# Layer 0's feed-forward in two-block form: nine of 22 up pairs as seven products, down sums carried over four parts

## The chip, the core and the metric

The kernel runs on one core of one Trainium2 chip. The metric is the device time of one execution in microseconds. A core has five engines that this text names as the profile does: PE is TensorE (matmuls; PEld is its weight load, which overlaps them), DVE is VectorE, ACT is ScalarE, POOL is GpSimd, and SP is SyncE, which issues nearly all DMAs here. Every engine works through its own instructions in a fixed order and waits on semaphores of the others.

## What is computed

Two model blocks in a row, on 256 tokens of width 1024. The change is in the second block's first layer, in its feed-forward, which runs over 512 tokens: 256 latent ones (tiles 0 and 1 of 128) and 256 of the context (tiles 2 and 3). Cut to that:

```python
def ada_norm(x, g, shift, scale):
    return rms_norm_2(x, g) * (1.0 + scale) + shift

def swiglu_ffn(h, w_in, w_out):
    a, g = jnp.split(h @ w_in, 2, axis=-1)
    return (jax.nn.silu(a) * g) @ w_out
...
    for i in range(DEPTH_2):
        mod_l = (silu_c @ ada_w[i] + ada_b[i])[:, None, :]
        mod_c = (silu_cc @ ada_w[i] + ada_b[i])[None, None, :]
        sh1_l, sc1_l, g1_l, sh2_l, sc2_l, g2_l = jnp.split(mod_l, N_MOD, axis=-1)
        ...
        h = h + g2_l * swiglu_ffn(ada_norm(h, norm_ffn[i], sh2_l, sc2_l), ffn_w_in[i], ffn_w_out[i])
        if ctx_out:
            hc = hc + g2_c * swiglu_ffn(ada_norm(hc, norm_ffn[i], sh2_c, sc2_c), ffn_w_in[i], ffn_w_out[i])
```

`w_in` is 1024 x 5632 and `w_out` is 2816 x 1024, so there are 22 pairs of up tiles (128 columns of `a` and the same 128 of `g`). The context's second half of a layer is needed in layer 0 alone.

## The kernel before, in words

**Numbers.** A product of float32 values is made from three matmuls of float32r values (`mm3`, lines 192 to 195): each operand is split into a rounded high part and the rest, and high x high, low x high and high x low are summed in PSUM. Weights come from DRAM in units of 128 x 1024 (512 KB) in one list, `UNITS`, in the order of their use. `w_load` (line 147) sends a unit into one of 5 `raw` buffers, `w_split` (line 161) makes `wh` on ScalarE (line 178) and `wl` on VectorE (line 179) in two of 12 `w` tiles, and `wnext` (line 181) hands the next unit out and keeps up to `cap` units split ahead.

**Layer 0's feed-forward.** It goes in two parts of 11 pairs. For each pair `ffn_up` (line 1122) runs 2 x 8 x 3 matmuls with a weight tile as the stationary operand and 512 tokens as the moving one, into two PSUM banks, and `ffn_act` (line 1109) makes silu(a) * g and splits it. The first two pairs (`ffn_up_first`, line 1132) do the context's half first, while the latent tokens are still being normed. `ffn_down0` (line 1149) then multiplies the part's 11 tiles by `w_out`, per output half and token tile, in a PSUM bank each, and `gated` (lines 1078 to 1081) multiplies a bank by the gate and adds it to the residual on VectorE. In part 0 all four token tiles go through one pass over the weights; in part 1 tiles 2 and 3 go first and tiles 0 and 1 in a second pass, so that the context's norm (`normed`, line 216, `to_T`, line 222) and layer 1's keys and values can begin early.

**The conditioning.** `ada_jobs` (line 293) computes the rows `silu(c) @ ada_w`, one vector of 1024 after the other, in 8 steps per vector: a DMA of 512 KB into one of two `a` buffers (line 304), and one pass of VectorE over it for each condition (line 324; for both c and c_ctx in layer 0 and for layer 1's first two, for c alone after). A vector's end adds the bias on GpSimd (line 339); the gate vectors (numbers 2 and 5) are also transposed on TensorE (line 348), sent to DRAM and read back as rows. The steps are strewn through the program by `ada_run`. The generator `adaC` holds the vectors (0,5), (1,0), (1,1) for both conditions and (1,3), (1,4), (1,2), (1,5) for one: 24 steps and 32.

**What sets the order.** In this stage the tile scheduler of the framework orders the instructions of every engine when the program is built. On the chip each engine then keeps to that order: an instruction that waits holds up all that stand behind it on its engine.

Of the kernel before, what the change touches and what calls it, by code (L numbers as in the profile page):

```python
# [14 lines left out]
ALU = mybir.AluOpType  # L15
# [12 lines left out]
NFT = FH // P  # L28
HALF = NFT // 2

# [6 lines left out]
def _units():  # L37

    u = [("f", "w_in", P * f) for f in range(8)]
    u += [("r", "w_in", k, 1024) for k in range(KD)]
    u += [("h", "w_in", 2 * k, 2048 + 512 * h) for h in range(2) for k in range(4)]
    u += [("r", "w_out", k, 0) for k in range(KD)]
    u += [("h", "ff1", 2 * k, 0) for k in range(4)] + [("f", "ff1", P * 4)]
    for f in range(NF):  # L50
        if 5 <= f + 2 < NF:
            u.append(("f", "ff1", P * (f + 2)))
        u.append(("r", "ff2", f, 0))
    v0 = [("h", "na_qkv", 2 * k, 2048) for k in range(4)]
# [6 lines left out]
    for part in range(2):  # L61
        for f in range(part * HALF, (part + 1) * HALF):
            u += [("f", "ffn_in0", P * f), ("f", "ffn_in0", FH + P * f)]
        dn = [("h", "ffn_out0", part * HALF + f, 512 * h) for h in range(2) for f in range(0, HALF, 2)]
        u += dn if part == 0 else dn + dn
# [18 lines left out]
def net(ctx, tc, x, xt, small, gk_up, gk_b, g_onorm, wst, final_norm, ctx_in, ctx_t, ada, ada_b, cvec,  # L84
# [76 lines left out]
    def w_split(upto):  # L161
        while wpos[1] < min(upto, len(UNITS)):
            i = wpos[1]
            raw = raws.pop(i)
            n = 512 if UNITS[i][0] == "h" and UNITS[i][1] == "ffn_out0" and (UNITS[i][2] % HALF) == HALF - 1 else 1024
            h = sb.tile([P, 1024], F32R, tag="w", bufs=NW, name=nm("wh"))
# [10 lines left out]
            else:  # L177
                A.copy(out=h[:, :n], in_=raw[:, :n])  # L178
                V.tensor_tensor(out=l[:, :n], in0=raw[:, :n], in1=h[:, :n], op=ALU.subtract)  # L179

    def wnext(kind):
        i = wpos[2]
# [9 lines left out]
    def mm3(o, lh, ll, rh, rl, first, last):  # L192
        T.matmul(o, lhsT=lh, rhs=rh, start=first, stop=False)  # L193
        T.matmul(o, lhsT=ll, rhs=rh, start=False, stop=False)  # L194
        T.matmul(o, lhsT=lh, rhs=rl, start=False, stop=last)  # L195

# [28 lines left out]

    def to_T_steps(xns, dst, t0, scale=None, bias=None):

        n = P * len(xns)
        for k in range(KD):
# [12 lines left out]
            else:  # L242
                r = t2([n])
                if k % 2:
# [31 lines left out]

    def mm_h(o, u, j, xp, t, first, last):
        h, l = u
        c = slice(j * 512, (j + 1) * 512)
        mm3(o, xp[0][:, t * P:(t + 1) * P], xp[1][:, t * P:(t + 1) * P], h[:, c], l[:, c], first, last)  # L280

# [818 lines left out]

    fT = new_T2()
    o_half(1, 2, hc, 1)
    xn = [normed(t) for t in hc]
    o_half(0, 0, lat, 0)
    o_half(1, 0, lat, 0, lambda: to_T(xn, fT, S, mod(0, 1, 4), mod(0, 1, 3)))
    xn = [normed(t) for t in lat]
# [14 lines left out]

    def ffn_up(L, src, n):
        ps_ = []
        for _ in range(2):
            u = wnext(("f", f"ffn_in{L}"))
            o = bank()
            for k in range(KD):
                mm_f(o[:, :n], u, src, k, 0, n, k == 0, k == KD - 1)
            ps_.append(o)
        return ffn_act(*ps_, n)  # L1130

    def ffn_up_first(src):

        us, os_ = [], []
        for _ in range(4):
            us.append(wnext(("f", "ffn_in0")))
            os_.append(bank())
            for k in range(KD):
                mm_f(os_[-1][:, S:N2], us[-1], src, k, S, S, k == 0, k == KD - 1)
        to_T(xn, src, 0, mod(0, 0, 4), mod(0, 0, 3))  # L1140
        z = []
        for n in range(4):
            for k in range(KD):
                mm_f(os_[n][:, 0:S], us[n], src, k, 0, S, k == 0, k == KD - 1)
            if n % 2:
                z.append(ffn_act(*os_[n - 1:n + 1], N2))
        return z

    def ffn_down0(hf, uu, tiles, between=None):
        ac = {t: bank() for t in tiles}  # L1150
        for f2 in range(0, HALF, 2):
            u = wnext(("h", "ffn_out0"))
            for j in range(min(2, HALF - f2)):
                f = f2 + j
                for t in tiles:
                    mm_h(ac[t], u, j, uu[f], t, f == 0, f == HALF - 1)
            ada_run(adaC)
            if f2 == 4 and between is not None:
                between()
        for t in tiles:  # L1160
            gated((lat + hc)[t], ac[t], 0, t // 2, 5, hf)

# [17 lines left out]

    for part in range(2):
        uu = []
        for f in range(HALF):
            if part == 0 and f < 2:
                uu += ffn_up_first(fT) if f == 0 else []
            else:
                uu.append(ffn_up(0, fT, N2))
            ada_run(adaC, 2)
        if part == 0:
            load_gates(0, 5)  # L1190
            for hf in range(2):
                ffn_down0(hf, uu, (2, 3, 0, 1))
        else:
            for hf in range(2):
                ffn_down0(hf, uu, (2, 3))
# [315 lines left out]

    load_gates(1, 5)
    nfb = [t2([512]) for _ in range(2)]
# [120 lines left out]
def _stream(w):  # L1634

    a = np.zeros((len(SLOT), P, 1024), np.float32)
    for s, i in SLOT.items():
# [9 lines left out]
        else:  # L1647
            k, c = s[2], s[3]
            n = 1 if s[1] == "ffn_out0" and k % HALF == HALF - 1 else 2
            a[i].reshape(P, 2, 512)[:, :n] = m[k * P:(k + n) * P, c:c + 512].reshape(n, P, 512).transpose(1, 0, 2)  # L1650
    return a
# [47 lines left out]
```

## Time and profile before

| | before |
|---|---|
| median of 3 runs | 1257.45 us (1257.27 to 1258.41) |
| the profiled execution | 1256.72 us |
| its span, first to last instruction | 1254.9 us |
| mean granted TensorE clock | 0.999 |
| layer 0's feed-forward, from its first matmul to layer 1's first | 557.8 to about 933.3 us of the span |

Times within a profile count from the span's start. In groups of instructions, what stands before the bar is what the instruction writes and reads, with its shape and count; behind it are the busy time in us, the mean of one in ns, the idle time of the engine just before, and what ended that. In a timeline a row starts with its start and its length in us. A matmul's printed length contains its way through the array, so that following ones overlap; the distance of their starts is what one takes.

### The profile page before, as it was taken

What the parts mean: (1) busy time and instruction counts of PE and PEld (TensorE: products, weight loads), DVE (VectorE), ACT (ScalarE), POOL (GpSimd) and SP (SyncE); (2) the same over time, 40 slices, a digit from 0 to 9 for tenths busy, and PEclk for the clock granted to TensorE, in tenths of its full rate; (3) what the DMA queues carried; (4) which work ended last, traced back from release to release, by engine and by line L of the source; (5) the groups of instructions that cost most, each with busy time, mean ns of one, the idle gap of its engine ahead of it and who ended that gap; (6) DMA issues with size and microseconds to landing.
All of it is one profiled execution on the core that took longest, in us unless ns stands there. A gap on an engine that the chain in (4) does not pass through costs nothing.

```text
span 1254.9 us, 18667 instructions
## 1 busy us (share of the span) xinstructions
PE 1244.0 (99%) x6872; PEld 1043.2 (83%) x6872; DVE 919.9 (73%) x1638; ACT 688.2 (55%) x1344; POOL 78.7 (6%) x137
## 2 busy tenths in 40 slices
PE   9999999999999999999999999999999999999997
PEld 8888889898888777789888888887888777999997
DVE  6959888697989887777877767633667988655555
ACT  8575655666549888655232222323456897544443
POOL 1010000030100000001000000000003220000000
PEclk9999999999999999999999999999999999999999
DMA  8647687787673333463656877633662324656650
GB/s 304 189 151 237 192 289 268 271 277 246 198 249 111 105 110 118 160 197 118 213 177 206 259 266 249 205 100 102 197 204 76 113 84 131 219 187 185 186 185 34
DMA packets 68507, 231.22 MB, mean 184 GB/s; under 512 B 8048, under 2 KB 8736, under 8 KB 68416
## 3 DMA queue, kind: packets, MB, share of 16 engines
q1 hardware_dynamic: 68128, 229.68, 57.0%
q8 instruction: 54, 0.88, 0.3%
q10 hardware_dynamic: 288, 0.35, 0.1%
q14 instruction: 37, 0.30, 0.1%
HBM read 228.93 MB, written 1.07 MB: 183 GB/s over the span
## 4 chain that ended last, share of the span: by engine, by line
PE 95%; ACT 2%; DVE 1%; issue 1%; DMA 0%; POOL 0%; SPq 0%; POOLq 0%; ACTq 0%
PE b L193 28%; PE b L194 28%; PE b L195 28%; PE b L1000 2%; PE b L1469 1%; PE b L981 1%; PE b L232 1%; PE b L1455 1%; PE b L562 1%; PE b L962 1%; PE b L963 1%; PE b L951 1%; PE b L1436 1%; DVE wl L179 0%; DMA t<-in_xt_dram 0%
## 5 line engine op out<-in xcount | busy, mean ns | idle before, releaser
L178 ACT CAST wh<-raw 128x1024 fp32r<-128x1024 f32 (+1 forms) x308 | 320.7, 1045 | 392.8 <-PE b L194 292.4
L179 DVE TENSOR_TENSOR wl<-raw,wh 128x1024 fp32r<-128x1024 f32 (+1 forms) x308 | 372.5, 1216 | 154.9 <-ACT wh L178 151.9
L193 PE MATMUL b<-t,wh 128*128 128x256 f32 (+1 forms) x1120 | 365.7, 327 | 0.0
L194 PE MATMUL b<-t,wl 128*128 128x256 f32 (+1 forms) x1120 | 365.6, 327 | 0.0
L195 PE MATMUL b<-t,wh 128*128 128x256 f32 (+1 forms) x1120 | 365.3, 327 | 0.0
L193 PE MATMUL b<-wh,t 128*128 128x512 f32 (+1 forms) x748 | 299.2, 402 | 1.2 <-ACT t L250 0.6
L194 PE MATMUL b<-wh,t 128*128 128x512 f32 (+1 forms) x748 | 294.8, 394 | 0.0
L195 PE MATMUL b<-wl,t 128*128 128x512 f32 (+1 forms) x748 | 294.7, 394 | 0.0
L193 PEld LDWEIGHTS b<-t,wh 128*128 128x128 f32 x1120 | 210.7, 188 | 22.2
L194 PEld LDWEIGHTS b<-t,wl 128*128 128x128 f32 x1120 | 210.8, 188 | 21.9
L195 PEld LDWEIGHTS b<-t,wh 128*128 128x128 f32 x1120 | 210.5, 188 | 20.4 <-DVE t L251 0.2
L195 PEld LDWEIGHTS b<-wl,t 128*128 128x128 f32 x748 | 140.4, 188 | 34.2
L193 PEld LDWEIGHTS b<-wh,t 128*128 128x128 f32 x748 | 140.4, 188 | 32.2 <-ACT t L250 1.0
L194 PEld LDWEIGHTS b<-wh,t 128*128 128x128 f32 x748 | 140.8, 188 | 30.1 <-DVE t L251 0.5
L324 DVE CUSTOM_DVE_ANT_0 a<-a,crow 128x1024 f32<-128x1024 f32 x96 | 117.6, 1233 | 28.8 <-DMA a<-in_ada_dram 28.3
L324 DVE CUSTOM_DVE_ANT_0 t<-a,crow 128x1024 bf16<-128x1024 f32 x64 | 78.5, 1237 | 7.3 <-DMA a<-in_ada_dram 7.1
L1112 DVE TENSOR_TENSOR t<-b,t 128x512 f32<-128x512 f32 (+1 forms) x42 | 23.7, 564 | 59.4 <-PE b L195 52.2
L205 POOL TENSOR_TENSOR c<-c,mhalf 128x1 f32<-128x1 f32 x21 | 14.2, 676 | 539.0 <-DVE c L204 538.9
L339 POOL TENSOR_TENSOR mod<-mod,bcol 128x8 f32<-128x8 f32 x20 | 13.4, 671 | 475.1 <-DVE mod L324 472.7
L1118 ACT CAST t<-t 128x512 fp32r<-128x512 f32 (+1 forms) x42 | 21.7, 516 | 28.6 <-DVE t L1112 28.6
L212 ACT ACTIVATE t<-t 128x512 f32<-128x512 f32 x40 | 24.8, 624 | 10.8 <-DVE t L1081 6.4
L1445 ACT ACTIVATE t<-b,c,c 128x512 f32<-128x512 f32 x32 | 26.0, 812 | 3.5 <-POOL c L1443 3.5
(244 smaller groups left out, 1212.6 us busy)
## 6 DMA issues: line engine op xcount, KB each, us to landing
raw<-in_wst_dram SPq DMA_DIRECT2D x310, 512.0 KB, 4.4
a<-in_ada_dram SPq DMA_DIRECT2D x96, 512.0 KB, 4.4
t<-in_rpb_dram SPq DMA_DIRECT2D x16, 256.0 KB, 4.5
t<-row SPq DMA_DIRECT2D x12, 256.0 KB, 5.1
t<-in_ctx_dram SPq DMA_DIRECT2D x8, 256.0 KB, 5.6
t<-in_xt_dram SPq DMA_DIRECT2D x4, 256.0 KB, 5.8
t<-in_x_dram SPq DMA_DIRECT2D x4, 256.0 KB, 6.5
crow<-in_cvec_dram SPq DMA_DIRECT2D x2, 512.0 KB
```

What stands on the lines that cost most here:

```text
L178: A.copy(out=h[:, :n], in_=raw[:, :n])
L179: V.tensor_tensor(out=l[:, :n], in0=raw[:, :n], in1=h[:, :n], op=ALU.subtract)
L193: T.matmul(o, lhsT=lh, rhs=rh, start=first, stop=False)
L194: T.matmul(o, lhsT=ll, rhs=rh, start=False, stop=False)
L195: T.matmul(o, lhsT=lh, rhs=rl, start=False, stop=last)
L205: G.tensor_tensor(out=ms[:, 3:4], in0=ms[:, 2:3], in1=mhalf[:, 0:1], op=ALU.pow)
L212: A.activation(out=junk[hf], in_=halves[hf], func=AF.Square, scale=1.0 / 32.0, accum_out=ms[:, hf:hf + 1])
L324: V.tensor_tensor_reduce(out=raw if ci == n_c - 1 else t2([D], BF16), in0=raw, in1=crow[ci], scale=1.0, scalar=0.0, op0=ALU.mult, op1=ALU.add,
L1000: T.matmul(po[e * 64:(e + 1) * 64, cols_], lhsT=v, rhs=probs[(head, "l" if lat_q else "c")][:, c, :], start=(c == 0), stop=(c == n_c - 1))
L1112: V.tensor_tensor(out=a, in0=pg_[:, :n], in1=a, op=ALU.mult)
L1118: A.copy(out=h, in_=a)
L1445: A.activation(out=pl, in_=sl, func=AF.Exp, scale=r, bias=mx[:, 1:2], accum_out=mx[:, 2:3])
```

## The change

1. **Seven products for eight.** For 9 of the 22 pairs (those of `SEVEN`) the product of a 2 x 2 block matrix (the columns of `a` and of `g`, by the two halves of the 1024 inputs) with a 2 x 2 block matrix (halves of the inputs, by latent and context tokens) is made from seven block products instead of eight, with sums of weight blocks (`pair_sums`) and of token blocks (`token_sums`, made once). A block product is 4 x 3 matmuls with 256 tokens. `ffn_up7` combines them from two reused banks and a third. The weight sums need 3.5 split units where a plain pair needs 2. Such pairs stand in turn with plain ones.
2. **Down sums in PSUM.** The 22 pairs go in four parts (6, 6, 6 and 4). Between parts the down sums are copied from PSUM to SBUF and back (`seed`), the matmuls add onto them, and the residual sum `gated` is made in the last part alone. Only the last part's down weights are read twice. `UNITS` has 26 down units where there were 36 (six of those of half size).
3. **Room.** The residual tiles go to DRAM at f = 2 (`put_away`, DMAs on ScalarE's queue) and come back in the last part (`fetch`, on SyncE's).
4. **Conditioning.** `adaC` ends with (1,2), 48 steps; one step is asked for at each pair except f = 3, one at the end of part 2 and six in the last part; what is left is emitted by `ada_run(adaC, 100)` before the last down group, as before. The vector (1,5) is a generator of its own, `adaD`, asked for in layer 1's feed-forward.

```diff
-HALF = NFT // 2
+PARTS = ((0, 6), (6, 12), (12, 18), (18, 22))
+SEVEN = (5, 7, 9, 11, 13, 15, 17, 19, 21)
...
+    def seven(u):
+        return u[1] == "ffn_in0" and u[2] % FH // P in SEVEN
...
-        while wpos[1] < len(UNITS) and wpos[1] - wpos[2] + 1 < cap[0]:
+        while wpos[1] < len(UNITS) and wpos[1] - wpos[2] + 1 < cap[0] and not seven(UNITS[wpos[1]]):
...
-    adaC = ada_jobs([(0, 5, True), (1, 0, True), (1, 1, True)] + [(1, v, False) for v in (3, 4, 2, 5)])
+    adaC = ada_jobs([(0, 5, True), (1, 0, True), (1, 1, True)] + [(1, v, False) for v in (3, 4, 2)])
+    adaD = ada_jobs([(1, 5, False)])
...
+    def pair_sums(f, got):
...
+        parts(x)
+        yield
+        V.tensor_tensor(out=z[:, a], in0=x[:, a], in1=y[:, a], op=ALU.add)
+        V.tensor_tensor(out=y[:, a], in0=y[:, a], in1=y[:, b], op=ALU.add)
+        parts(y)
+        yield
+        V.tensor_tensor(out=z[:, b], in0=z[:, a], in1=y[:, b], op=ALU.add)
+        parts(z)
+        yield
+        V.tensor_tensor(out=x[:, a], in0=z[:, b], in1=x[:, b], op=ALU.add)
...
+    def ffn_up7(got, conv):
+        wpos[2] += 2
+        r, q, g = [bank()[:, 0:S] for _ in range(3)]
...
+        def prod(o, n, c, X, first=True):
+            h, l = got[n]
+            for j in range(H):
+                k = slice(c + j * P, c + (j + 1) * P)
+                mm3(o, h[:, k], l[:, k], *X(j), first and j == 0, j == H - 1, not first)
...
+        prod(r, 0, 0, lambda j: a(0, j))
+        A.copy(out=c1[:, 0, :], in_=r)
+        prod(q, 1, 0, lambda j: sT[(3, j)])
+        A.copy(out=c3[:, 0, :], in_=q)
+        run(conv)
+        prod(r, 2, 512, lambda j: sT[(2, j)], False)
+        A.copy(out=c3[:, 1, :], in_=r)
+        prod(g, 0, 512, lambda j: a(0, H + j))
+        got[0] = None
+        V.tensor_tensor(out=c1[:, 0, :], in0=g, in1=c1[:, 0, :], op=ALU.add)
+        A.activation(out=c1[:, 0, :], in_=c1[:, 0, :], func=AF.Silu)
+        run(conv)
+        prod(r, 2, 0, lambda j: sT[(1, j)], False)
...
+    def seed(b, t, hf):
+
+        if (t, hf) in dsum:
+            A.copy(out=dbank[b], in_=dsum[(t, hf)])
...
-            ada_run(adaC, 2)
...
+            if f != 3:
+                ada_run(adaC)
...
+            for hf in range(2):
+                ffn_down0_last(hf, uu, (2, 3), 1)
+                for i in range(2):
+                    seed(2 * hf + i, i, hf)
+            fetch(lat, 0)
             xn = [normed(t) for t in hc]
-            ffn_down0(0, uu, (0, 1))
+            ffn_down0_last(0, uu, (0, 1), 1)
+            dsum.clear()
             bT2 = new_T2()
             ada_run(adaC, 100)
             cap[0] = 7
-            ffn_down0(1, uu, (0, 1), lambda: to_T(xn, bT2, S, mod(1, 1, 1), mod(1, 1, 0)))
+            ffn_down0_last(1, uu, (0, 1), 0, lambda: to_T(xn, bT2, S, mod(1, 1, 1), mod(1, 1, 0)))
...
+        if f < 12:
+            ada_run(adaD)
+        if f == 12:
+            load_gates(1, 5)
```

Three places in the built order. The changed file's lines are 5 higher in the helpers: `mm3` is 198 to 200, the ada step 329 (an ISA row), the gate's transposition 353, the norm's transposition 237, `to_T`'s scaling and low part 253 and 256, the weight split 180.

TensorE before, in the down group of part 1: the transposition of the vector (1,5), `mod_8195`, adaC's last.

```order
L193 MATMUL b_8431<-wh_8390,t_7886 128x512
L194 MATMUL b_8431<-wh_8390,t_7887 128x512
L195 MATMUL b_8431<-wl_8391,t_7886 128x512
L348 MATMUL b_8470<-cm,mod_8195 8x128
L193 MATMUL b_8430<-wh_8434,t_7964 128x512
L194 MATMUL b_8430<-wh_8434,t_7965 128x512
```

TensorE after, at the end of the last part: its last down matmuls (`b_6843`), the transposition of (1,2), `mod_9373`, now adaC's last, and the first transpositions of the context's norm.

```order
L198 MATMUL b_6843<-wh_9293,t_9116 128x512
L199 MATMUL b_6843<-wh_9293,t_9117 128x512
L200 MATMUL b_6843<-wl_9294,t_9116 128x512
L353 MATMUL b_9399<-cm,mod_9373 8x128
L237 MATMUL b_9464<-cm,t_9252 128x128
L237 MATMUL b_9464<-cm,t_9261 128x128
```

The gate's transposition moved from the middle of a down group to the place between the last down matmul and the norm that follows it.

VectorE before, where the context's norm for layer 1 is split into high and low parts.

```order
L179 TENSOR_TENSOR wl_8940<-raw_8827,wh_8939 128x1024
L251 TENSOR_TENSOR t_8792<-t_8905,t_8791 128x256
L248 TENSOR_SCALAR t_8912<-b_8909,mod_7006,mod_6674 128x256
L179 TENSOR_TENSOR wl_8958<-raw_8845,wh_8957 128x1024
L251 TENSOR_TENSOR t_8794<-t_8912,t_8793 128x256
L179 TENSOR_TENSOR wl_8976<-raw_8863,wh_8975 128x1024
```

VectorE after, in two pieces: the weight splits ahead of the last 17 steps of adaC, and the last of those steps with what follows (`mod_9373` is (1,2), `mod_11319` is (1,5) of adaD).

```order
L329 ISA a_9337,mod_9209<-a_9337,crow_87 128x1024
L329 ISA mod_9209 128x1
L180 TENSOR_TENSOR wl_9431<-raw_9410,wh_9430 128x1024
L180 TENSOR_TENSOR wl_9449<-raw_9416,wh_9448 128x1024
L329 ISA a_9340,mod_9209<-a_9340,crow_87 128x1024
```

```order
L329 ISA a_9390,mod_9373<-a_9390,crow_87 128x1024
L329 ISA mod_9373 128x1
L329 ISA a_11315,mod_11319<-a_11315,crow_87 128x1024
L329 ISA mod_11319 128x1
L253 TENSOR_SCALAR t_9467<-b_9464,mod_8498,mod_7458 128x256
L256 TENSOR_TENSOR t_9319<-t_9467,t_9318 128x256
L329 ISA a_11317,mod_11319<-a_11317,crow_87 128x1024
```

No ada step stood near this norm before; now 17 steps of adaC stand one behind the other ahead of it, and adaD's stand among its rows.

VectorE after, inside the pair of seven products of f = 7 (the combinations L1245 to L1258, and between them L1197, the splits for the pair of seven that comes next).

```order
L1245 TENSOR_TENSOR t_7137<-b_7136,t_7137 128x256
L1197 TENSOR_TENSOR wl_7282<-raw_7084,wh_7281 128x1024
L1250 TENSOR_TENSOR t_7138<-b_7134,t_7139 128x256
L1197 TENSOR_TENSOR wl_7288<-raw_7086,wh_7287 128x1024
L1253 TENSOR_TENSOR t_7137<-b_7135,t_7139 128x256
L1197 TENSOR_TENSOR wl_7322<-raw_7280,wh_7321 128x1024
L1255 TENSOR_TENSOR t_7138<-t_7138,t_7137 128x256
L1258 TENSOR_TENSOR t_7138<-b_7134,t_7137 128x256
```

VectorE before had per pair the two rows of `ffn_act` and two weight splits:

```order
L179 TENSOR_TENSOR wl_7188<-raw_7046,wh_7187 128x1024
L1112 TENSOR_TENSOR t_7077<-b_7052,t_7077 128x512
L179 TENSOR_TENSOR wl_7223<-raw_7094,wh_7222 128x1024
L1119 TENSOR_TENSOR t_7081<-t_7077,t_7080 128x512
L324 ISA t_7086,mod_7003<-a_7008,crow_87 128x1024
```

The splits of a pair of seven now stand a pair ahead of their use.

More of the change, by code (lines that the diff above doesn't have):

```diff
@@ L60, in _units @@
     u += o + o
-    for part in range(2):
-        for f in range(part * HALF, (part + 1) * HALF):
+    for lo, hi in PARTS:
+        for f in range(lo, hi):
             u += [("f", "ffn_in0", P * f), ("f", "ffn_in0", FH + P * f)]
-        dn = [("h", "ffn_out0", part * HALF + f, 512 * h) for h in range(2) for f in range(0, HALF, 2)]
-        u += dn if part == 0 else dn + dn
+        dn = [("h", "ffn_out0", f, 512 * h) for h in range(2) for f in range(lo, hi, 2)]
+        u += dn if hi < NFT else dn + dn
     kv = [("h", "gqa_qkv", 2 * k, D) for k in range(4)]
@@ L190, in wnext, with mm3 @@
         return convs.pop(i)
[L192 to L195, printed above, removed]
+    def mm3(o, lh, ll, rh, rl, first, last, onto=False):
+        T.matmul(o, lhsT=lh, rhs=rh, start=first, stop=False, skip_group_check=onto)
+        T.matmul(o, lhsT=ll, rhs=rh, start=False, stop=False, skip_group_check=onto)
+        T.matmul(o, lhsT=lh, rhs=rl, start=False, stop=last, skip_group_check=onto)
     def inv_root(o, ms, n, eps=EPS):
@@ L1101, in net @@
     fT = new_T2()
+    fX = [t2([2, S]) for _ in range(KD)]
     o_half(1, 2, hc, 1)
@@ new lines, in net, with put_away, fetch @@
+    dsum, kept = {}, {}
+    def put_away(rows, t0):
+        for t, halves in enumerate(rows):
+            for hf in range(2):
+                kept[(t0 + t, hf)] = dr.tile([P, 512], F32, name=nm("res"))
+                nc.scalar.dma_start(out=kept[(t0 + t, hf)], in_=halves[hf])
+                halves[hf] = None
+    def fetch(rows, t0):
+        for t, halves in enumerate(rows):
+            for hf in range(2):
+                halves[hf] = t2([512])
+                nc.sync.dma_start(out=halves[hf], in_=kept[(t0 + t, hf)])
@@ new lines, in net, with ffn_down0 @@
+    dbank = []
+    def seed(b, t, hf):
+        if (t, hf) in dsum:
+            A.copy(out=dbank[b], in_=dsum[(t, hf)])
+    def ffn_down0(hf, uu, last):
+        onto = (0, hf) in dsum
+        for f2 in range(0, len(uu), 2):
+            u = wnext(("h", "ffn_out0"))
+            for t in range(4):
+                for j in range(2):
+                    f = f2 + j
+                    mm_h(dbank[t], u, j, uu[f], t, f == 0 and not onto, f == len(uu) - 1, onto)
+                if f2 + 2 == len(uu):
+                    if not onto:
+                        dsum[(t, hf)] = t2([512])
+                    A.copy(out=dsum[(t, hf)], in_=dbank[t])
+                    if not (hf and last):
+                        seed(t, t, 1 - hf)
+        if hf and last:
+            for t in (2, 3):
+                for half in range(2):
+                    seed(2 * half + t - 2, t, half)
+            ada_run(adaC)
@@ L1159, in ffn_down0, with ffn_down0_last @@
+    def ffn_down0_last(hf, uu, tiles, n_ada, between=None):
+        for f2 in range(0, len(uu), 2):
+            u = wnext(("h", "ffn_out0"))
+            for i, t in enumerate(tiles):
+                for j in range(2):
+                    f = f2 + j
+                    mm_h(dbank[2 * hf + i], u, j, uu[f], t, False, f == len(uu) - 1, True)
+            if n_ada:
+                ada_run(adaC, n_ada)
+            if f2 == 2 and between is not None:
                 between()
-        for t in tiles:
-            gated((lat + hc)[t], ac[t], 0, t // 2, 5, hf)
+        for i, t in enumerate(tiles):
+            gated((lat + hc)[t], dbank[2 * hf + i], 0, t // 2, 5, hf)
```

130 lines of the change are left out of this document (99 added, 31 removed).

## The prediction

> **What bounds the kernel now.** I read the page first: the busy shares, then the chain that ended last.
>
> ```profile
> PE 1244.0 (99%) x6872; PEld 1043.2 (83%) x6872; DVE 919.9 (73%) x1638; ACT 688.2 (55%) x1344; POOL 78.7 (6%) x137
> PE 95%; ACT 2%; DVE 1%; issue 1%; DMA 0%; POOL 0%; SPq 0%; POOLq 0%; ACTq 0%
> ```
>
> TensorE is busy for 99% of the span and carries 95% of the chain. So matmul time that is taken out is time won, as long as nothing makes TensorE wait; and any new wait is paid in full. Then the stage itself, layer 0's feed-forward, by windows (columns: us, PE, PEld, DVE, ACT, POOL busy with counts, granted clock, DMA share, GB/s):
>
> ```profile
> 557.80:933.30 375.50, 375.50 (x1717) 306.37 (x1716) 246.00 (x356) 121.56 (x170) 12.88 (x26) 1.00 0.60 190
> ```
>
> TensorE has no gap in 375.5 us at full clock; VectorE works 246 of them (66%), ScalarE 122. What a matmul costs is its distance to the next start, not its printed duration. The timeline of TensorE, 8 starts apart with 256 columns and 4 apart with 512:
>
> ```profile
> 573.75 0.28 PE L193 MATMUL b<-t,wh 128*128 128x256 f32 x1
> ...
> 574.69 0.28 PE L195 MATMUL b<-t,wh 128*128 128x256 f32 x1
> ...
> 588.02 0.39 PE L193 MATMUL b<-t,wh 128*128 128x512 f32 x1
> ...
> 588.95 0.39 PE L194 MATMUL b<-t,wl 128*128 128x512 f32 x1
> ```
>
> That is 0.1175 us for 256 columns and 0.2325 us for 512: half the columns, half the time.
>
> **The products.** A plain pair is 2 tiles x 8 x 3 = 48 matmuls of 512 columns, 11.16 us. A pair of seven products is 7 x 4 x 3 = 84 matmuls of 256 columns, 9.87 us. Nine pairs save 9 x 1.29 = **11.6 us**. The down projection keeps its 528 matmuls; seeding its sums is left to ScalarE. The Trainium skill's page "TensorE: Matmul & The Clock Gate", section "Back-to-back issue gap", speaks against this: it gives a sustained 131 ns at 512 columns and 81 ns at 128, so (my estimate by a straight line) 98 ns at 256, and a seven-product pair would be 1.9 us dearer than a plain one. The rows above disagree at both widths.
>
> **VectorE beside the products.** Durations, by form (columns behind the bar: busy us, mean ns, idle before):
>
> ```profile
> L179 DVE TENSOR_TENSOR wl<-raw,wh 128x1024 fp32r<-128x1024 f32 x74 | 90.5, 1222 | 42.5 <-ACT wh L178 40.9
> L324 DVE CUSTOM_DVE_ANT_0 a<-a,crow 128x1024 f32<-128x1024 f32 x56 | 67.8, 1223 | 28.7 <-DMA a<-in_ada_dram 28.3
> L1119 DVE TENSOR_TENSOR t<-t,t 128x512 fp32r<-128x512 f32 x22 | 15.1, 687 | 0.2
> L1081 DVE TENSOR_TENSOR t<-t,t 128x512 f32<-128x512 f32 x16 | 10.7, 685 | 0.0
> ...
> L1112 DVE TENSOR_TENSOR t<-b,t 128x256 f32<-128x256 f32 x20 | 8.5, 425 | 16.5 <-PE b L195 16.5
> L804 ACT ACTIVATE t<-b 128x256 f32<-128x256 f32 x28 | 10.6, 378 | 4.0 <-PE b L195 4.0
> ```
>
> For one plain and one seven-product pair together VectorE does: 3.5 splits of sums (3 x 1.22 + 0.69 = 4.35), four weight sums (4 x 0.685 = 2.74), two plain splits (2.44), the plain activation (1.38), five half-width combinations and the last split (5 x 0.425 + 0.69 = 2.8), and two ada steps for both conditions (4 x 1.22 = 4.9): 18.6 us beside 9.87 + 11.16 = 21.0 us of TensorE, 89%. So VectorE is not the bound, but close to it. In the order its splits stand a whole pair ahead of their use. The shortest cover is inside a seven: the product into r by the second half of weight sum 2 ends, four matmuls (0.47 us) follow, and then r is overwritten; its copy takes 0.38 us on ScalarE plus the hand-overs. I give each seven 0.3 us of wait, **+3 us** in all, between 0 and the 1.4 us of one product each (12.6 us). The token sums (four times 4 x 0.425 + 2 x 0.69, 12.3 us) stand before the first seven in part 0, whose pairs cover them; without that cover they would cost that.
>
> **The conditioning steps: the dear term.** Before, ada_run takes two steps at each of 22 pairs and one at each down unit of part 0, so its 56 steps end early. After, adaC has 48 steps and 28 calls of one step; the other 20 are emitted at once by ada_run(adaC, 100), just ahead of the last down group. In VectorE's order all 24 single-condition steps, vectors (1,3), (1,4) and (1,2), come after the first residual sum of the last part (L1086), and 17 of them after a weight split (wl_9449) that needs a tile of the last down unit. In TensorE's order the transposition of (1,2) (L353) stands directly behind the last down matmul, ahead of the norm's transpositions (L237) and of everything in layer 1. TensorE therefore stops there until the last of the 24 steps is done. Before, the same transposition (L348) stood in the middle of the down group, its input finished long ago.
>
> What a step costs in a row, from VectorE's timeline and from the rows of tile a in the same stretch (its loads, line 304):
>
> ```profile
> 782.09 1.23 DVE L324 CUSTOM_DVE_ANT_0 a<-a,crow 128x1024 f32<-128x1024 f32 x1 [1.06 <-DMA a<-in_ada_dram]
> ...
> 796.64 1.22 DVE L324 CUSTOM_DVE_ANT_0 a<-a,crow 128x1024 f32<-128x1024 f32 x1 [1.32 <-DMA a<-in_ada_dram]
> ...
> 802.25 1.23 DVE L324 CUSTOM_DVE_ANT_0 a<-a,crow 128x1024 f32<-128x1024 f32 x1 [0.90 <-DMA a<-in_ada_dram]
> L304 SPq DMA_DIRECT2D a<-in_ada_dram x19: 327/328/328, 741.1 to 797.9; - x19
> DMA to landing us min/median/max: 3.6/4.4/5.5
> ```
>
> From 782.09 to 802.25 there are 7 steps, 2.88 us each, and VectorE idles before them for the load. The two buffers explain it: a load starts when the step two before it has ended, so two steps take one landing plus one operation. (4.4 + 1.22) / 2 = 2.8 us with the median, 2.4 with the shortest, 3.4 with the longest; 1.22 us if no load held it up. I take 2.8. The Trainium skill's page "DMA: Bandwidth & Descriptors", section "Anatomy of one DMA — SWDGE (gpsimd) path", fits 2.0 us plus bytes / 436 GB/s, 3.2 us for these 512 KB (on another issuing path). By that a step would take 2.2 us and the total below would be some 18 us lower; no landing here is as short.
>
> Now from the end U of the last seven's seventh product. TensorE has 86 matmuls of the last part to run, 20.0 us. VectorE has, in its order before the first of the 24 steps, six operations of ada steps for both conditions (7.3), four splits (4.9), four half rows (2.7) and the combination (1.1): 16 us. Then 24 x 2.8 = 67.2 us; the other work among them (13.9 us of sums, norm and splits) goes for the most part into the 1.6 us in which each step waits for its load. So the last step ends at U + 83.2, and TensorE, done at U + 20.0, stands for **63.2 us**. (That the seeds of the last group also wait for L1086, some 5 us, lies inside this.)
>
> Behind the wait, the plain course is in the rows of before:
>
> ```profile
> 944.35 0.40 PE L195 MATMUL b<-wl,t 128*128 128x512 f32 x1
> 944.59 1.91 PE L232 MATMUL b<-cm,t 128*128 128x128 f32 x16
> 946.25 0.48 PE L193 MATMUL b<-wh,t 128*128 128x512 f32 x1
> L205 POOL TENSOR_TENSOR c<-c,mhalf 128x1 f32<-128x1 f32 x21 | 14.2, 676 | 539.0 <-DVE c L204 538.9
> L219 DVE TENSOR_SCALAR t<-t,c 128x512 f32<-128x512 f32 x22 | 9.8, 486 | 6.8 <-POOL c L205 6.8
> ```
>
> Context keys and values take 48 x 0.2325 = 11.2 us, the latent tokens' transpositions 1.7 us more (944.59 to 946.25), and another 1.7 us go to the context's: 14.6 us. After, the eight loads of adaD come early in SyncE's order and its eight steps are strewn among the rows of this norm on VectorE: six before the last low part (L256) of the context tokens, two more before the latent norm's scaling (L224). 8 x 2.8 = 22.4 us, less 1 for a load already under way, then four scalings (1.9), the second root on GpSimd (0.7), the transpositions (1.7) and a first split (0.4): 26 us from the last step of adaC to the first latent matmul. That is **+11.4 us** over the plain course. Past it nothing is late: adaD's row is needed only in the last feed-forward.
>
> **The sum** is made against the profiled execution, 1256.72 us (span 1254.9 and 1.8 around it; 0.7 under the median of 1257.45): 1256.7 - 11.6 + 3 + 63.2 + 11.4 = 1322.7, so **1322 us**. Shortest landings take off 24 x 0.4 + 8 x 0.4 = 13 and the sevens' wait 3 (1307); longest add 24 x 0.6 + 5 = 19 (1342).
>
> **Rivals.**
> 1. The up stage becomes VectorE's. 89% load, each new operation in a fixed order: if each seven loses a whole product (1.4 us), 1332; with some part borders too, 1335. For it: the 0.47 us cover. Against it: splits stand a pair ahead. 12%.
> 2. The loads don't pace the steps: 24 x 1.22 = 29.3 and then the 13.9 us no longer hide; 16 + 29.3 + 13.9 - 20 = 39.2 us of wait, and about 1 behind it: 1288. Against it: 28.3 us of idle time before L324 for loads. 5%.
> 3. The other side: faster, because the 24 steps are through when TensorE gets there. Place: L353 behind the last down matmul; price: the wait only; 1256.7 - 11.6 + 3 = 1248. It decides if the wait and what follows stay under 8.6 us. Against it: VectorE's order puts 16 us and 24 operations of 1.22 us behind U, where TensorE has 20 us left; for it, only that the engines might not follow that order. 4%.
> 4. Narrow matmuls are bounded by their weight load:
>
> ```profile
> L193 PEld LDWEIGHTS b<-t,wh 128*128 128x128 f32 x383 | 72.1, 188 | 14.8
> ```
>
> 84 x 0.188 = 15.8 us a pair, 4.6 more than plain: +41 in place of -11.6, 1375. Starts 0.1175 us apart speak against it. 1%. (That half the columns don't make half the time is also what the Trainium skill's page on TensorE, cited above, says.)
>
> **How the numbers follow.** My forecast's case holds 78%. The range reaches from 1300 (short landings, and a little toward rival 2) to 1338 (long ones, and rival 1). Faster by over 0.2%, which is about what a measurement of this kernel can tell from no change: 4%, rival 3. Within 0.2%: 1%. Slower: 95%.
>
> **What would show it.** Right: in the profile after, one gap of TensorE of some 60 us before L353, released by GpSimd's L344 and that by VectorE's ada steps, 2.4 to 2.9 us apart and each waiting for its load; a seven of 9.9 to 10.2 us; TensorE's busy time near 1232 us, 93 to 94% of the span. Wrong: no long wait at L353, or ada steps that run without waiting for loads, or gaps of several us within the sevens.

## The result, and the profile after

The changed kernel takes 1323.44 us (median of 4 runs, 1322.13 to 1325.44) where before takes 1257.93 (4 runs): a ratio of 1.0522, 95% interval 1.0503 to 1.054. It is slower by 65.5 us; 1322 was forecast. The profiled execution takes 1323.32 us with a span of 1321.5.

The page first, busy shares and the chain that ended last:

```profile
PE 1242.6 (94%) x7196; PEld 1056.4 (80%) x7196; DVE 961.4 (73%) x1726; ACT 738.2 (56%) x1444; POOL 76.2 (6%) x137
PE 84%; DMA 7%; DVE 6%; ACT 2%; issue 2%; POOL 1%; SPq 0%; POOLq 0%; DVEq 0%; ACTq 0%
```

TensorE fell from 99% of the span to 94%, and 13% of the chain are now loads and VectorE. Where it stands, by windows from the first matmul of layer 0's feed-forward to its last down matmul, from there to row L353, and from L353 to the first latent matmul (columns: us, then PE, PEld, DVE, ACT, POOL busy with counts, granted clock, DMA share, GB/s), and by the waits of TensorE in the whole stretch (us in total, times, longest):

```profile
558.09:929.53 371.44, 366.21 (x2023) 313.62 (x2021) 245.56 (x373) 168.53 (x261) 8.73 (x22) 0.99 0.46 145
929.53:986.12 56.59, 0.16 (x2) 0.00 (x1) 31.83 (x50) 1.04 (x1) 0.60 (x3) 0.54 0.70 225
986.12:1012.02 25.90, 19.73 (x82) 15.54 (x82) 20.09 (x42) 9.33 (x25) 1.46 (x3) 0.83 0.52 164
```

```profile
PE b L353 <- POOL mod L344: 56.4, 1, 56.4
PE b L198 <- ACT b L1287: 5.2, 1, 5.2
PE b L237 <- DVE t L224: 4.0, 2, 3.3
PE b L198 <- DVE t L253: 1.6, 1, 1.6
```

One stop of 56.4 us at the transposition of (1,2), named after GpSimd's bias (L344); GpSimd is busy for 0.6 us of it, so the cause lies further back. The chain of waits has it, in order of time (start, us, what; the rows of 0.1 us or less between these are left out):

```profile
944.88 4.51 DMA a<-in_ada_dram
949.53 1.23 DVE a L329
950.79 4.10 DMA a<-in_ada_dram
955.03 1.23 DVE a L329
956.29 4.43 DMA a<-in_ada_dram
960.85 1.22 DVE a L329
```

A landing and an operation take turns: a step's end frees its buffer, and the load of the step after the next starts into it. VectorE's own rows show the same (in brackets the idle time before), with the rows of tile a:

```profile
946.54 1.22 DVE L329 CUSTOM_DVE_ANT_0 a<-a,crow 128x1024 f32<-128x1024 f32 x1 [1.68 <-DMA a<-in_ada_dram]
...
984.55 1.22 DVE L329 CUSTOM_DVE_ANT_0 a<-a,crow 128x1024 f32<-128x1024 f32 x1 [1.56 <-DMA a<-in_ada_dram]
DMA to landing us min/median/max: 3.5/4.2/4.9
```

From 946.54 to 984.55 there are 14 steps, 2.72 us each; (4.2 + 1.23) / 2 is 2.72. The nine before them, from 918.69 on, come 3.09 us apart, since sums, norm and weight splits stand among them.

The pairs, from TensorE's timeline: the start of a plain pair, of the pair of seven products behind it, and of the plain pair after that, with the place inside the seven:

```profile
660.82 0.40 PE L198 MATMUL b<-t,wh 128*128 128x512 f32 x1
...
672.06 0.28 PE L198 MATMUL b<-t,wh 128*128 128x256 f32 x1
...
677.76 0.28 PE L198 MATMUL b<-t,w 128*128 128x256 f32 x1
678.03 0.38 PE L198 MATMUL b<-t,wh 128*128 128x256 f32 x1
678.25 0.28 PE L199 MATMUL b<-t,wl 128*128 128x256 f32 x1
...
682.28 0.40 PE L198 MATMUL b<-t,wh 128*128 128x512 f32 x1
```

11.24 us for the plain pair, 10.22 for the seven (the five sevens that stand in one piece take 10.17 to 10.22). Inside it two starts lie 0.27 and 0.22 us apart instead of 0.12: there the bank r is overwritten, and TensorE's weight load waits for ScalarE's copy of it (L1242).

### The profile page after: what moved, and what is told of

It is laid out like the page before. It is cut to its first block, busy times and chain, and to the rows that moved or that the text cites. A ratio compares the mean times of both kernels' runs of the same rounds, so it can differ in the third digit from the quotient of the medians.

```text
span 1321.5 us, 19513 instructions
## 1 busy us (share of the span) xinstructions
PE 1242.6 (94%) x7196; PEld 1056.4 (80%) x7196; DVE 961.4 (73%) x1726; ACT 738.2 (56%) x1444; POOL 76.2 (6%) x137
## 4 chain that ended last, share of the span: by engine, by line
PE 84%; DMA 7%; DVE 6%; ACT 2%; issue 2%; POOL 1%; SPq 0%; POOLq 0%; DVEq 0%; ACTq 0%
PE b L198 24%; PE b L199 24%; PE b L200 24%; DMA a<-in_ada_dram 6%; DVE a L329 2%; PE b L1006 2%; PE b L1657 1%; PE b L987 1%; PE b L1643 1%; DVE wl L180 1%; PE b L237 1%; PE b L568 1%; DVE t L329 1%; PE b L968 1%; PE b L969 1%
## 5 line engine op out<-in xcount | busy, mean ns | idle before, releaser
L180 DVE TENSOR_TENSOR wl<-raw,wh 128x1024 fp32r<-128x1024 f32 x280 | 341.3, 1226 | 181.4 <-ACT wh L179 126.9
L179 ACT CAST wh<-raw 128x1024 fp32r<-128x1024 f32 x280 | 293.4, 1052 | 230.5 <-PE b L199 159.1
L198 PE MATMUL b<-t,wh 128*128 128x256 f32 (+1 forms) x1192 | 370.7, 311 | 0.0
L199 PE MATMUL b<-t,wl 128*128 128x256 f32 (+1 forms) x1192 | 369.4, 310 | 0.0
L200 PE MATMUL b<-t,wh 128*128 128x256 f32 (+1 forms) x1192 | 369.1, 310 | 0.0
L198 PEld LDWEIGHTS b<-t,wh 128*128 128x128 f32 x1192 | 224.4, 188 | 18.4 <-ACT t L1242 1.2
L199 PEld LDWEIGHTS b<-t,wl 128*128 128x128 f32 x1192 | 224.6, 188 | 15.5
L200 PEld LDWEIGHTS b<-t,wh 128*128 128x128 f32 x1192 | 224.2, 188 | 14.0 <-DVE t L1179 0.2
L1196 ACT CAST wh<-raw 128x1024 fp32r<-128x1024 f32 x27 | 28.4, 1052 | 55.5 <-PE b L199 29.6
L1197 DVE TENSOR_TENSOR wl<-raw,wh 128x1024 fp32r<-128x1024 f32 x27 | 32.9, 1218 | 31.0 <-ACT wh L1196 30.9
L353 PE MATMUL b<-cm,mod 128*8 128x128 f32 x6 | 1.4, 289 | 56.4 <-POOL mod L344 56.4
L344 POOL TENSOR_TENSOR mod<-mod,bcol 128x8 f32<-128x8 f32 x20 | 9.9, 493 | 650.1 <-DVE mod L329 648.8
L353 PEld LDWEIGHTS b<-cm,mod 128*8 128x8 f32 x6 | 0.5, 84 | 57.2 <-POOL mod L344 56.9
```

Source lines behind the costliest of these rows:

```text
L198: T.matmul(o, lhsT=lh, rhs=rh, start=first, stop=False, skip_group_check=onto)
L199: T.matmul(o, lhsT=ll, rhs=rh, start=False, stop=False, skip_group_check=onto)
L200: T.matmul(o, lhsT=lh, rhs=rl, start=False, stop=last, skip_group_check=onto)
L1196: A.copy(out=h, in_=r)
L1197: V.tensor_tensor(out=l, in0=r, in1=h, op=ALU.subtract)
```

## The experiments

Each is one kernel with its edit against the changed kernel, or against the run it names. Runs with one time only have a profile of that execution beside it; the four times of the changed kernel lie 3.3 us apart, so a single time tells no difference smaller than that.

**Is it the row L353, or VectorE's order?** turn_late moves only the end of (1,2), its bias and transposition, and with it the reading of its row (`load_gates`):

```diff
-            ada_run(adaC, 100)
+            ada_run(adaC, 20)
...
-    load_gates(1, 2)
     acx = kv_pass((2, 3))
+    ada_run(adaC, 100)
+    load_gates(1, 2)
```

> The changed kernel with only the end of vector (1,2), its bias and transposition, moved from ahead of the last down group to behind layer 1's keys and values of the context; all steps stay. Theory: the steps in VectorE's order are what holds, not the one row L353; the wait goes over to the norm's transpositions, whose scaling on VectorE stands behind the same steps, and ends about when some 27 of the 32 steps are done: U + 92 us or so for the first latent matmul where it was U + 110, so 1300 to 1310 us. Rival (the row L353 alone holds TensorE): 56 us less, 1267.

Measured: 1307.45 us (one run), in the range. TensorE's waits in the stretch:

```profile
PE b L353 <- POOL mod L344: 26.7, 1, 26.7
PE b L237 <- DVE t L253: 13.5, 2, 10.8
PE b L198 <- ACT b L1287: 5.7, 1, 5.7
```

The keys and values of the context (11 us) now run inside the row of steps, which accounts for most of the 16 us; but the norm's scalings (L253) stand behind steps as well, and L353 stops TensorE again, later. The first latent matmul starts 91.4 us after the last seven's last product (901.63 to 993.05), where 92 was expected. The row of steps is the cause, and L353 only the first place where it shows.

**How many steps lie behind the last pair?** six_calls:

```diff
+            if onto and hf:
+                ada_run(adaC)
```

in `ffn_down0`, ahead of each unit's matmuls.

> The changed kernel with six more calls of adaC, at the three down units of the second half in parts 1 and 2; adaD as it is. In VectorE's order 7 single-condition steps of adaC are then left behind the last pair (24 before). Theory: 7 x 2.8 = 20 us and some 8 us of other work against TensorE's 20, a wait of about 8 us before L353 in place of 56; adaD's 13 us stay: 1262 to 1275. Rival (the steps cost their own 1.22 us each on a full VectorE, wherever they stand): six of 48 moved, not over 15 us less, 1308 or more.

Measured: 1271.57 us (one run), in the range; the wait at L353 is larger than worked out:

```profile
PE b L353 <- POOL mod L344: 13.3, 1, 13.3
```

Six more calls, for a generator of 48 steps, took away 52 us, and no step is left out. So it isn't the steps' work that costs, but their place: 17 of the 24 single-condition steps went ahead of the last sums in VectorE's order, and 7 are left behind them. That a step called earlier lets those behind it in the generator move up too is the likely reason; no run varies it.

**Do two buffers set the pace?** three_bufs:

```diff
-    NT2 = 58
+    NT2 = 56
...
-                loaded[n] = sb.tile([P, D], F32, tag="ada", bufs=2, name=nm("a"))
+                loaded[n] = sb.tile([P, D], F32, tag="ada", bufs=3, name=nm("a"))
```

> The changed kernel with three ada buffers in place of two, and two t tiles fewer to make room (56 for 58). Theory (two buffers make the load pace the steps): three steps take a landing plus an operation, (4.3 + 1.23) / 3 = 1.84 us in place of 2.8; the 24 steps of the row give back 22 us and adaD's eight up to 7, so 1288 to 1302 us. Rival (VectorE's other work or the transfers' rate paces the steps): no change beyond 5 us, 1318 or more.

Measured: 1303.89 us (one run): 19.5 less than the changed kernel, 2 us over the upper end. Its wait, its steps and its rows of tile a:

```profile
PE b L353 <- POOL mod L344: 40.3, 1, 40.3
```

```profile
946.08 1.23 DVE L329 CUSTOM_DVE_ANT_0 a<-a,crow 128x1024 f32<-128x1024 f32 x1
...
966.97 1.23 DVE L329 CUSTOM_DVE_ANT_0 a<-a,crow 128x1024 f32<-128x1024 f32 x1 [1.95 <-DMA a<-in_ada_dram]
```

```profile
DMA to landing us min/median/max: 3.4/4.6/5.6
```

Ten steps in 20.9 us, 2.09 each (2.72 with two buffers). The buffers pace the steps. The forecast of 1.84 us a step took a landing of 4.3 us; with three in flight it is 4.6, and (4.6 + 1.23) / 3 = 1.94. The other 0.15 us a step stays open. The edit also takes two t tiles, so that not every microsecond need be the buffer's.

**What are the 11.4 us behind L353?** ada_d_late:

```diff
-                if (L, v) == (0, 0) and k < 2:
-                    G.tensor_copy(out=loaded[n][:, 0:1], in_=crow[k][:, 0:1])
+                if (L, v) in ((0, 0), (1, 5)) and k < 2:
+                    G.tensor_copy(out=loaded[n][:, 0:1], in_=(act[-1] if L else crow[k])[:, 0:1])
...
-        a = t2([n])
+        a = t2([n]); act.append(a)
```

with `act` an empty list at the start.

> The changed kernel with one thing other: the first two loads of adaD wait for an activation of layer 1's third pair of up tiles, so that its eight steps leave the rows of the context's norm. Theory: the 13 us that the way from L353 to the first latent matmul is longer than before are mostly adaD's steps; without them that way takes about 15 us in place of 26, so 1310 to 1315 us. Rival (the norm's own chain behind L353 and TensorE's lower clock after the long stop make the 13 us): 1319 or more.

Measured: 1313.84 us (one run), 9.6 less; the wait at L353 is still 56.5, and from L353 to the first latent matmul it takes 17.3 us (985.64 to 1002.98) in place of 25.9. So adaD's eight steps in the norm's rows are 8.6 of the 11.4 us by these rows (9.6 by the whole time, one run each). The other 2.7 are in the same run's rows: its first 16 transpositions behind L353 take 3.5 us (985.81 to 989.33) and the second 16 take 2.3 (1000.64 to 1002.98), where the forecast had 1.7 for each.

**Does the length of the last down group count?** long_end_flush:

```diff
-PARTS = ((0, 6), (6, 12), (12, 18), (18, 22))
+PARTS = ((0, 4), (4, 10), (10, 16), (16, 22))
```

> The changed kernel with one thing other: parts of 4, 6, 6 and 6 pairs in place of 6, 6, 6 and 4; conditioning as it is, 24 steps behind the last pair. Theory: the stop at L353 is the row's 67 us and 16 of VectorE's before it, less what TensorE still has to do; its down matmuls behind the last pair go from 86 to 134, 11 us more cover, so 11 us less: 1309 to 1315 us. Rival (the wait is a fixed time from the last down matmul on, as when the flush only starts there): no change, 1321 or more.

Measured: 1314.49 us (one run), 9.0 less:

```profile
PE b L353 <- POOL mod L344: 53.6, 1, 53.6
PE b L198 <- ACT b L1287: 0.5, 1, 0.5
```

The stop at L353 shrank by only 2.8 us and the one for the seeds by 4.7: the longer group seems to take up the one before it reaches the other. Together with the 1.8 us of TensorE's lower clock behind the seeds' stop, which goes as well, that is 9.3 of the 11 us of cover that were expected.

**What is left without the row of steps?** spread takes the edit of ada_d_late and

```diff
+            ada_run(adaC)
...
-                ada_run(adaC)
+                ada_run(adaC, 2 if f >= 12 and f not in SEVEN else 1)
```

(the first in `ffn_down0` at each unit, the second at each pair); spread_plain is the same with `SEVEN = ()`; the second edit then asks for two steps at every pair from f = 12 on, so that its steps come earlier still.

> The changed kernel with 23 more calls of adaC ahead of the last part (one at each down unit of parts 0 to 2, a second at the plain pairs from f = 12 on), and adaD tied to the third pair of layer 1's feed-forward; nothing is left out. Theory: the whole slow-down is the row of steps behind the last pair and adaD's eight among the norm's rows; without them what is left is the seven products, so 1257.9 - 11.6 + 0 to 3 = 1246 to 1249 us, no PE gap before L353. Rival (the up stage is VectorE's, the steps only show it): 18 to 23 more operations of 1.22 us beside the pairs and down groups make TensorE wait there, 1255 or more.

> As the run with the spread steps, but SEVEN is empty: all 22 pairs plain, the four parts and the seeds kept. Theory: the seven products are the only gain and the four parts cost nothing, so 1257.9 with 0 to +2, and 11.6 (10 to 12) over the run with the sevens. Rival (the seeds or the parts cost or gain of themselves): it differs from before by over 3 us, and the sevens' share is then not 11.6.

Measured: spread 1257.87 us (10 runs, ratio to before 1.0003, interval 0.9994 to 1.0013), spread_plain 1260.66 (8 runs, 1.0028, 1.0017 to 1.0039). The stop before (1,2)'s transposition and adaD's steps in the norm are gone, and with them 65.6 us of the changed kernel's time. But both forecasts fell. Spread came out at its rival's number, though not in the rival's way: no pair of the up stage waits. And spread_plain is 2.7 us over before, where 0 to 2 was forecast, and only 2.8 over spread, where it was 10 to 12. Spread's TensorE has one stop in part 0's down group, at the transposition of (0,5), which the new calls brought near its steps:

```profile
644.83 0.39 PE L200 MATMUL b<-wl,t 128*128 128x512 f32 x1
647.86 0.38 PE L353 MATMUL b<-cm,mod 128*8 128x128 f32 x1 [2.64 <-POOL mod L344]
647.88 0.78 PE L198 MATMUL b<-wh,t 128*128 128x512 f32 x1
648.46 0.63 PE L199 MATMUL b<-wh,t 128*128 128x512 f32 x1
648.89 0.63 PE L200 MATMUL b<-wl,t 128*128 128x512 f32 x1
```

2.64 us of wait, and 7 matmuls behind it 0.43 us apart instead of 0.23, 1.4 us more. Most of the rest is the sevens' 10.2 us instead of 9.87, as in the changed kernel (nine times 0.35 at most), and the norm behind the last down matmul, which spread_plain shows alone: from the feed-forward's first matmul to the latent tokens' transpositions it takes 389.0 us (557.92 to 946.93), before 386.8 (557.82 to 944.59). So the four parts, cut as they are here, cost some 2 us. Together these are 9.4 us over 1246.3. Of the 2 us that are left, 1.4 lie behind the stage (from the latent tokens' transpositions to the end it is 311.7 us in spread, 310.3 before), with no cause shown. The stop of 2.64 us is not in spread_plain. With the 1.4 us behind it, the sevens' 3.2 us and a wait of the norm that is 1.3 us longer in spread (1.6 for 0.3), it makes up nearly all that the two runs came closer together than was forecast.

spread_2 leaves part 0 as the changed kernel has it:

```diff
+            if onto:
+                ada_run(adaC, 2 if last else 1)
```

in place of spread's call in `ffn_down0`. spread_2_long_end adds the parts of long_end_flush to it, long_end_plain has `SEVEN = ()` besides, and long_end_one has `ada_run(adaC)` for the line above.

> As the run spread, but without the calls at part 0's down units, and with two at each down unit of part 2: all steps stay. Theory: of what spread lost against 1247, 4.2 us lie at the transposition of (0,5) in part 0's down group (a wait of 2.8 us and the lower clock behind it), which this leaves as the changed kernel has it; 1252.5 to 1255 us, faster than before by 0.2 to 0.4%. Rival (the added steps cost elsewhere as much): 1257 or more.

> As spread_2, with parts of 4, 6, 6 and 6 pairs in place of 6, 6, 6 and 4. Theory: in spread and spread_plain the context's transpositions, scalings and 3.5 us of waits stand bare behind the last down matmul, since the last down group is two units long; with three units they lie inside it, as before the change. 3 to 4 us under spread_2: 1249 to 1251.5 us. Rival (the bare norm is due to the order of the two passes, not to the group's length): within 1 us of spread_2.

> As spread_2_long_end, but SEVEN is empty: all 22 pairs plain. Theory: nine pairs of seven products are worth 9 x 1.35 = 12 us of matmul time less some 0.3 us each where TensorE passes between the widths and 2 us of waits behind steps, so 7 to 9.5 us over spread_2_long_end: 1259.5 to 1262 us. Rival (the gain came from the longer last group and the spread alone): within 3 us of 1252.5.

> As spread_2_long_end, with one call of adaC at each down unit of part 2 in place of two: all steps stay. Theory: TensorE's three waits of 0.5 to 1.1 us in part 2's down group and behind it come from steps ahead of the weight splits on VectorE; with fewer there 0 to 2 us go: 1250.5 to 1252.5 us. Rival (the steps that now come later make the last group wait): 1253.5 or more.

Measured: spread_2 1257.13 us (10 runs, ratio to before 1.0002, 0.9993 to 1.0011), the rival's number: the 2.6 us went at (0,5) and came back as a wait of 3.3 us in the first seven behind part 2's down group, with 1.5 us of lower clock behind it (that seven takes 14.97 us). VectorE's and ScalarE's rows there, of spread_2:

```profile
863.17 1.23 DVE L329 CUSTOM_DVE_ANT_0 a<-a,crow 128x1024 f32<-128x1024 f32 x1 [1.42 <-DMA a<-in_ada_dram]
...
871.27 1.23 DVE L329 CUSTOM_DVE_ANT_0 a<-a,crow 128x1024 f32<-128x1024 f32 x1 [1.24 <-DMA a<-in_ada_dram]
...
873.56 0.68 DVE L1119 TENSOR_TENSOR t<-b,t 128x512 f32<-128x512 f32 x1
```

```profile
874.28 0.62 ACT L1125 CAST t<-t 128x512 fp32r<-128x512 f32 x1 [5.00 <-DVE t L1119]
874.80 0.36 ACT L1237 COPY t<-b 128x256 f32<-128x256 f32 x1
```

It is the same chain on a small scale: steps at their loads' pace stand ahead of the plain pair's activation on VectorE, ScalarE stands for that, and the copy that frees the seven's bank is late. The others: spread_2_long_end 1252.5 (5 runs, 0.996, 0.9946 to 0.9974), 1.0 over the upper end of its forecast; long_end_plain 1258.91 (10 runs, 1.0012, 1.0002 to 1.0021), 0.6 under the lower end; long_end_one 1251.6 (4 runs, 0.995, 0.9934 to 0.9967), in its range. The waits of TensorE in this stage, of spread_2 and of long_end_one:

```profile
PE b L198 <- ACT t L1237: 3.3, 1, 3.3
PE b L237 <- DVE t L253: 1.6, 1, 1.6
PE b L198 <- DVE t L253: 0.9, 1, 0.9
```

```profile
PE b L198 <- ACT t L1237: 0.7, 1, 0.7
PE b L237 <- DVE t L224: 0.7, 1, 0.7
PE b L198 <- DVE t L1250: 0.3, 1, 0.3
```

The longer last group hides the context's norm again: its waits for L253, 2.5 us in spread_2, are gone, in spread_2_long_end too. That run is 4.6 us under spread_2, but not all of it is the norm: its wait for L1237 is 1.0 us in place of 3.3. The plain versions say less for the group: 1.8 us from spread_plain to long_end_plain, whose calls differ as well. What is left of the sevens' gain is 6.4 us between long_end_plain and spread_2_long_end, a little under the range expected, though the plain one's second calls stand at more pairs, as in spread_plain. long_end_one is the fastest version here, 0.5% under before; the 0.9 us to spread_2_long_end lie within the runs' scatter (1250.18 to 1252.07 against 1251.63 to 1252.89).

## Why the prediction was right

By its terms, each against the trace:

| term | forecast | measured |
|---|---|---|
| nine pairs of seven products, with their waits | -11.6 + 3 = -8.6 | 9 x (10.22 - 11.24) = -9.2 |
| TensorE stands until the last step of adaC | +63.2 | 5.2 (seeds) + 1.8 (clock behind it) + 56.4 = +63.4 |
| the way from there to the first latent matmul | 26 for 14.6, +11.4 | 25.9, +11.3 |
| sum | +66.0 | +65.5; the spans differ by 66.6 |

The measured terms are the whole of the stage: from the feed-forward's first matmul to the first latent matmul it takes 453.9 us (558.09 to 1012.02), before 388.4 (557.82 to 946.25). The other 1.1 us of the spans lie ahead of it (0.3) and behind it (0.8).

**The products.** Half the columns cost half the time, as the rows of before said. The wait inside a seven was put at 0.3 us and at the bank r; a seven is 0.35 us longer than worked out, 0.25 of it there, and the rest is starts 0.119 us apart in place of 0.1175. The up stage did not become VectorE's: no wait of a pair in the changed kernel is over 0.3 us (rival 1). Nor does the weight load bound the narrow matmuls: by rival 4 a seven would take 15.8 us.

**The row of steps.** The forecast had the last step end 83.2 us after the last seven's last product; that product's last matmul ends at about 901.9, and the bias behind the last step starts at 985.86, so 84.0. The steps were put at 2.8 us throughout, with the other work hidden in their waits. Measured, the first nine come 3.09 us apart and the last 2.72: the other work is hidden only in part, and the free pace is a little faster than taken. That the two errors cancel, so that the end lies within 1 us of the forecast, is luck; the mechanism isn't. three_bufs shows that the pace is the two buffers'. turn_late and six_calls show that VectorE's order is the cause and not the single row of TensorE. Rival 2 (no pacing, 1288) falls with the wait for a load before each of the last 15 steps, rival 3 (through in time, 1248) with the stop of 56.4 us. By the Trainium skill's page "DMA: Bandwidth & Descriptors", section "Anatomy of one DMA — SWDGE (gpsimd) path", whose fit for DMAs issued from GpSimd makes 3.2 us of such a load (an estimate), the sum would have been some 18 us lower. The median landing here, of loads issued from SyncE, is 4.2 us, and 4.6 with three in flight.

**Behind it.** adaD's eight steps were worth 8.6 us of this way when ada_d_late took them out. The 2.7 us that remain there are longer transpositions: 1.8 us in the first 16, which run at the lower clock behind the stop (below), and 0.6 in the second. The forecast had put all 11.4 on the steps and the norm's operations, and nothing on the clock.

**What was not in the forecast, though its sum came out.** Two things stand in the changed kernel. One is TensorE's lower clock behind a stop, 1.8 us after the seeds' and 1.6 in the matmuls behind L353. The forecast of TensorE's busy time failed, 1232 us where the page has 1242.6: the waits of 0.1 to 0.2 us inside the sevens count as busy, and so does every matmul's longer time at the lower clock. With the sevens' 3.2 us these are some 6.6 of the 10.6 us; the norm's transpositions, longer too, are not counted in. The other is the seeds' wait of 5.2 us: it was put inside the 63.2 us, which is right here, since the row of steps ends later. A third shows only without the row: the last down group is too short to hide the context's norm, 2.2 to 2.5 us (389.0 for 386.8 in spread_plain; 386.5 in long_end_plain, 558.18 to 944.72).

## What to carry to other kernels

Count the calls of a generator of background work against its steps whenever the stage that carries it is recut: what is left over is emitted at once, and if a late transposition or a norm stands behind it in the order of an engine, all of it is on the path. The price of such a row here was not its operations but about (landing + operation) / buffers for each step, and moving six calls gave more (52 us) than making the steps faster (19.5). The product with fewer multiplications did gain, but a quarter of the 12.3 us that it removed (nine times the 1.37 from 11.24 to 9.87) went into longer sevens, most of it at one short copy between two uses of a bank; and the four parts cost some 2 us where the last group had become too short to cover what follows.

## What the runs showed of the hardware

TensorE's clock drops at or within a short stop and takes 3 to 4 us of work to come back; behind L353, where more waits follow, it took 9 (986.12 to 995.2). Behind the 5.23 us stop for the seeds, the changed kernel's timeline has

```profile
916.35 0.80 PE L198 MATMUL b<-wh,t 128*128 128x512 f32 x1 [5.23 <-ACT b L1287]
916.94 0.63 PE L199 MATMUL b<-wh,t 128*128 128x512 f32 x1
917.37 0.63 PE L200 MATMUL b<-wl,t 128*128 128x512 f32 x1
917.80 0.63 PE L198 MATMUL b<-wh,t 128*128 128x512 f32 x1
```

starts 0.43 us apart in place of 0.23, for nine matmuls. Behind the 2.64 us stop of spread there were seven such, and behind L353's 56.4 us eight besides the transpositions. Behind the 3.28 us stop of spread_2 the matmuls have 256 columns, and their starts lie 0.21 us apart in place of 0.12, for some twelve:

```profile
875.22 0.58 PE L198 MATMUL b<-t,wh 128*128 128x256 f32 x1 [3.28 <-ACT t L1237]
875.60 0.42 PE L199 MATMUL b<-t,wl 128*128 128x256 f32 x1
875.82 0.41 PE L200 MATMUL b<-t,wh 128*128 128x256 f32 x1
```

In these four places a stop cost 1.4 to 1.8 us beyond its own length. The granted clock shows it: 1.00 from 646 to 647 us, inside spread's stop, and 0.50 from 648 to 651 behind it; 1.00 from 873 to 874 in spread_2's stop, and 0.50 from 875 to 878. Its mean over the 9 us around either stop is 0.81, which makes 3.4 us at half clock; over the 12 us around the seeds' stop it is 0.72, twice that.

The length of the stop alone doesn't decide. Spread and spread_2 have the same three short waits ahead of the context's keys and values (1.6, 0.5 and 0.9 us, with two transpositions behind each of the first two). Behind them spread runs on at full clock, and spread_2 doesn't: from 932 to 937 us the granted clock is 1.00 and 0.66. The second matmul there, of spread and then of spread_2:

```profile
933.13 0.39 PE L199 MATMUL b<-wh,t 128*128 128x512 f32 x1
933.29 0.63 PE L199 MATMUL b<-wh,t 128*128 128x512 f32 x1
```

The Trainium skill's page "TensorE: Matmul & The Clock Gate", section "What's actually happening", has a window of 3.4 us that runs freely and a low clock after at least one idle window. The stretches of 3.4 us and the same waits falling either way agree with the free window; that it takes a whole idle one does not fit spread's 2.64 us stop, and there the trace decides. The same page's section "Wait — 56ns, not 53.3ns?" of the Trainium skill gives 426.7 ns at 512 columns for the cold array, which these rows show; for the warm one it gives 215.7 ns, where the rows here show 0.2325 us, and the rows decide.
